# Coarser DMAs in a convolution kernel: stores and residual loads of three image pairs, and the last two pairs stored whole

## Chip, cores, metric

One core of one Trainium2 chip. The metric is device time in microseconds (us) of one execution. One run of the kernel before (211.6 us, slow) is left out by the comparison. A DMA is carried out by 16 DMA engines, here mostly in packets of 16 KB; it has landed when all 16 engines have sent their completion. Times inside an execution are counted from the start of the profiled span, which is 1.8 to 1.9 us shorter than the device time.

## The reference

A 3x3 convolution with padding 1 over 16 images of 64 channels and 64x64 pixels, plus a residual, all in float32.

```python
def reference(x, weight, residual):      # x (16,64,64,64), weight (64,64,3,3), residual (16,64,64,64)
    x_pad = np.pad(x, ((0, 0), (0, 0), (pad, pad), (pad, pad)), mode='constant')
    for b ...: for co ...: for ci ...: for kh ...: for kw ...:
        output[b, co] += weight[co, ci, kh, kw] * x_pad[b, ci, kh:kh+h, kw:kw+w]
    return (output + residual).astype(np.float32)
```

## The kernel before

Images go in pairs, 2 MB a pair, on 128 partitions. Three buffers (`xr`) take the loads of x. ScalarE casts every image in two halves into bfloat16 (`xp`, four buffers), TensorE convolves it into PSUM, and VectorE adds PSUM to the residual, which lies in one large tile (`ro`) for all eight pairs; the sum stays there and is stored from there. SyncE issues nearly all DMAs, in program order, on one queue.

```python
EARLY = (slice(0, 2), slice(2, 4), slice(4, 6), slice(6, 7))      # pairs stored while the work goes on
RES = (                                # pairs, columns, "issue behind the load of x pair ..."
    (slice(0, 1), WHOLE, None), (slice(1, 2), WHOLE, 1), (slice(2, 4), WHOLE, 3),
    (slice(4, 6), WHOLE, 5), (slice(6, 7), WHOLE, 7),
    (slice(7, 8), LEFT, 7), (slice(7, 8), RIGHT, 7),
)
# ... SyncE:
for p in range(NPAIR):
    if p >= NXR:                                        # NXR = 3 buffers
        nc.sync.wait_ge(s_half, 2 * (p - NXR) + 3)      # first cast of image 2*(p-3)+2 has ended
    load_x(p)                                           # (p == 0 goes to the front of the program)
    for i, (_, _, behind) in enumerate(RES):
        if behind == p:
            load_ro(i, nc.sync)
wait_ro(nc.sync, len(RES) - 2)                          # left half of residual pair 7 has landed
for pairs in EARLY:
    nc.sync.wait_ge(s_add, 2 * pairs.stop + 1)
    store(pairs).then_inc(s_out, 16)
# ... ScalarE, image n = 2p + im (cut):
i = nc.scalar.copy(out=t[64:128, 0:J, :], in_=x4[hp, :, 0, :])
i.then_inc(s_half, 1)
nc.scalar.copy(out=t[0:64, 1 : J + 1, :], in_=x4[hp, :, 1, :]).then_inc(s_pack, 1)
# ... at the very end, after all adds:
for cols in (LEFT, RIGHT):
    store(slice(NPAIR - 1, NPAIR), cols)
```

The load of x pair 7 (x7 below) reuses the buffer of pair 4, whose last reader is the second cast of image 9. But the counter `s_half` counts only first casts, so x7 waits for the first cast of image 10, which is the first image of pair 5. That cast can only run when x5 has landed.

Of the kernel before, what the change touches and what calls it, by code (L numbers as in the profile page):

```python
# [15 lines left out]
def kernel(  # L16
# [15 lines left out]
    NPAIR = B // 2  # L32
# [3 lines left out]
    NXR = 3  # L36
    NXP = 4
    NZERO = 4 + 2 * NXP
    EARLY = (slice(0, 2), slice(2, 4), slice(4, 6), slice(6, 7))
    WHOLE, LEFT, RIGHT = slice(0, NPIX), slice(0, NPIX // 2), slice(NPIX // 2, NPIX)  # L40
    RES = (
        (slice(0, 1), WHOLE, None),
        (slice(1, 2), WHOLE, 1),
        (slice(2, 4), WHOLE, 3),
        (slice(4, 6), WHOLE, 5),
        (slice(6, 7), WHOLE, 7),
        (slice(7, 8), LEFT, 7),
        (slice(7, 8), RIGHT, 7),
    )
# [40 lines left out]
    def wait_ro(e, i):  # L90
        e.wait_ge(s_r[i % NR], 16 * (i // NR + 1))

    def store(pairs, cols=slice(0, NPIX)):
        return nc.sync.dma_start(out=out_bc[:, pairs, cols], in_=ro[:, pairs, cols])
# [47 lines left out]
    with tc.tile_critical(no_gpsimd_drain=True):  # L142
# [14 lines left out]
        wait_ro(nc.sync, len(RES) - 2)  # L157
        for pairs in EARLY:
            nc.sync.wait_ge(s_add, 2 * pairs.stop + 1)
# [23 lines left out]
        for n in range(B):  # L183
            p, im = divmod(n, 2)
# [25 lines left out]
        for n in range(B):  # L210
            p, im = divmod(n, 2)
# [43 lines left out]
                m.then_inc(s_conv, 1)  # L255


    for cols in (LEFT, RIGHT):
        store(slice(NPAIR - 1, NPAIR), cols)
    with tc.tile_critical(sync_engine=mybir.EngineType.Pool, no_gpsimd_drain=True):  # L260
        nc.gpsimd.wait_ge(s_out, 16 * len(EARLY))
        tc.free_semaphores([s_w, *s_x, *s_r, s_out, s_id, s_half, s_pack, s_bank, s_conv, s_add])
# [30 lines left out]
```

## Time and profile before

| | |
|---|---|
| time | 122.21 us, median of 3 (122.2 to 122.54) |
| span of the profiled execution | 120.6 us |
| bytes | 33.70 MB read, 16.78 MB written, 22 DMAs |
| busy | PE 87.7 us, VectorE 76.0 us, ScalarE 63.1 us |

### The profile page before, as it was taken

The page shows a single profiled execution, that of the slowest core. Times are in us where ns is not written, and L with a number is a line of the kernel's source. Part 1 is how long each engine was busy: PE and PEld are TensorE (multiplying, and loading weights), DVE is VectorE, ACT ScalarE, POOL GpSimd, SP SyncE. Part 2 cuts the span into 40 slices and gives each one's busy share as a digit, 9 for nine tenths or more (in the row PEclk, how much of TensorE's full clock was granted, in tenths as well). Part 3 has the DMA queues.
Part 4 walks back from the last instruction along what each step waited for, and adds up shares of the span by engine and source line. Part 5 has one row for each costly group of instructions (what it writes and reads, how often), then busy time and mean ns, then how long its engine had stood idle before and what let it go on. Part 6 is the DMA issues. An engine that isn't in the chain of part 4 may idle for free.

```text
span 120.6 us, 734 instructions
## 1 busy us (share of the span) xinstructions
PE 87.7 (73%) x389; PEld 10.7 (9%) x105; DVE 76.0 (63%) x40; ACT 63.1 (52%) x37; POOL 2.4 (2%) x16
## 2 busy tenths in 40 slices
PE   0000609999999999999999999999999999400000
PEld 0000300111101110101010101010101010000000
DVE  0000080039898898988989898898988989890000
ACT  4001999999988595875959578595800000000000
POOL 5200000000000000000000000000000000000000
PEclk9999999999999999999999999999999999995555
DMA  7999999999999999999999999999999999999994
GB/s 239 429 424 429 430 429 429 429 435 435 435 429 429 424 429 424 429 435 424 435 429 435 435 435 418 421 459 435 429 429 429 429 429 435 435 435 429 399 427 168
DMA packets 3808, 50.48 MB, mean 419 GB/s; under 512 B 352, under 2 KB 480, under 8 KB 480
## 3 DMA queue, kind: packets, MB, share of 16 engines
q1 hardware_dynamic: 3664, 48.38, 94.2%
q10 hardware_dynamic: 144, 2.10, 4.1%
HBM read 33.70 MB, written 16.78 MB: 419 GB/s over the span
## 4 chain that ended last, share of the span: by engine, by line
PE 71%; DVEq 2%; DVE 2%; issue 0%
PE ps L101 54%; PE ps L100 17%; DVEq L142 2%; DVE ro L220 2%
## 5 line engine op out<-in xcount | busy, mean ns | idle before, releaser
L220 DVE TENSOR_TENSOR ro<-ps,ro 64x2048 f32<-64x2048 f32 x32 | 73.2, 2288 | 17.7 <-PE ps L101 17.2
L101 PE MATMUL ps<-xp,wl 128*128 128x504 bf16 (+1 forms) x288 | 80.0, 388 | 0.2
L190 ACT CAST xp<-xr 64x2048 bf16<-64x2048 f32 x16 | 30.3, 1896 | 22.5 <-PE ps L101 13.1
L100 PE MATMUL ps<-xp,wl 128*128 128x504 bf16 (+1 forms) x92 | 35.9, 390 | 3.4 <-PEq L241 3.4
L194 ACT CAST xp<-xr 64x2048 bf16<-64x2048 f32 x16 | 30.4, 1898 | 0.4
L100 PEld LDWEIGHTS ps<-xp,wl 128*128 128x128 bf16 x96 | 9.5, 99 | 79.1 <-issue 79.1
L206 DVE CAST wl<-ps 32x192 bf16<-32x192 f32 x8 | 2.8, 348 | 14.9 <-PE ps L233 14.8
L233 PE MATMUL ps<-ident,wraw 128*32 128x128 f32 x9 | 2.1, 412 | 12.6 <-DMA wraw<-in_weight_dram 12.6
L233 PEld LDWEIGHTS ps<-ident,wraw 128*32 128x32 f32 x9 | 1.2, 137 | 13.0 <-issue 12.6
L190 ACT ACT_TABLE_LOAD x1 | 1.3, 1283 | 1.1 <-SPq L142 1.1
L199 ACT CAST wl<-ps 32x192 bf16<-32x192 f32 x4 | 1.2, 306 | 0.0
L177 POOL MEMSET xp<- 64x64 bf16 x4 | 0.6, 146 | 0.2
L176 POOL MEMSET xp<- 64x64 bf16 x4 | 0.6, 144 | 0.2
L165 POOL TENSOR_SCALAR_AFFINE_SELECT ident<-ident 128x128 f32<-128x128 f32 x1 | 0.3, 292 | 0.2 <-POOL ident L163 0.2
L179 POOL MEMSET wl<- 64x192 bf16 x1 | 0.3, 253 | 0.1
L178 POOL MEMSET wl<- 64x192 bf16 x1 | 0.3, 251 | 0.1
L163 POOL MEMSET ident<- 128x128 f32 x1 | 0.2, 204 | 0.7 <-SPq L142 0.7
L277 POOL MEMSET const-bfloat16-1.0<- 128x1 bf16 x1 | 0.1, 111 | 0.0
L277 POOL MEMSET const-uint8-127<- 128x1 uint8 x1 | 0.1, 111 | 0.0
L277 POOL MEMSET const-float32-1.0<- 128x1 f32 x1 | 0.1, 108 | 0.0
L277 POOL MEMSET const-float32-0.0<- 128x1 f32 x1 | 0.1, 103 | 0.2 <-issue 0.2
## 6 DMA issues: line engine op xcount, KB each, us to landing
xr<-in_x_dram SPq DMA_DIRECT2D x8, 2048.0 KB, 14.4
out_dram<-ro SPq DMA_DIRECT2D x3, 4096.0 KB, 19.2
ro<-in_residual_dram SPq DMA_DIRECT2D x2, 4096.0 KB, 20.7
ro<-in_residual_dram SPq DMA_DIRECT2D x2, 2048.0 KB, 18.1
ro<-in_residual_dram ACTq DMA_DIRECT2D x1, 2048.0 KB, 12.0
ro<-in_residual_dram SPq DMA_DIRECT2D x2, 1024.0 KB, 18.8
out_dram<-ro SPq DMA_DIRECT2D x1, 2048.0 KB, 13.7
out_dram<-ro SPq DMA_DIRECT2D x2, 1024.0 KB, 9.4
```

The costliest lines, as they stand in the source:

```text
L100: return e.matmul(out=out_, lhsT=lhsT, rhs=rhs, start=start, stop=stop, skip_group_check=True)
L101: return e.add_instruction(mybir.InstMatmult(name=nc.get_next_instruction_name(), engine=PE, ins=[e.lower_ap(rhs), e.lower_ap(lhsT)], outs ...
L142: with tc.tile_critical(no_gpsimd_drain=True):
L176: nc.gpsimd.memset(t[0:64, 0, :], 0.0).then_inc(s_id, 1)
L177: nc.gpsimd.memset(t[64:128, J, :], 0.0).then_inc(s_id, 1)
L190: i = nc.scalar.copy(out=t[64:128, 0:J, :], in_=x4[hp, :, 0, :])
L194: nc.scalar.copy(out=t[0:64, 1 : J + 1, :], in_=x4[hp, :, 1, :]).then_inc(s_pack, 1)
L199: i = nc.scalar.copy(**weight_block(h, *b))
L206: i = nc.vector.tensor_copy(**weight_block(h, *b))
L220: i = nc.vector.tensor_tensor(out=o4[hp, :, par, :], in0=psj[64 * par : 64 * par + 64, :, :], in1=o4[hp, :, par, :], op=ADD)
L233: i = nc.tensor.transpose(out=tp[0:32, t // 3, 128 * (t % 3) : 128 * (t % 3) + 128], in_=wraw3[:, :, t], identity=ident[:, :])
L277: nc = _bacc.Bacc("TRN2", target_bir_lowering=False, num_devices=1)
```

## The change

The intent is fewer, larger DMAs on a kernel bound by transfers: 19 instead of 22.

```diff
-    EARLY = (slice(0, 2), slice(2, 4), slice(4, 6), slice(6, 7))
+    EARLY = (slice(0, 3), slice(3, 6))
@@ RES
         (slice(2, 4), WHOLE, 3),
-        (slice(4, 6), WHOLE, 5),
-        (slice(6, 7), WHOLE, 7),
+        (slice(4, 7), WHOLE, 4),
         (slice(7, 8), LEFT, 7),
         (slice(7, 8), RIGHT, 7),
@@ the end
-    for cols in (LEFT, RIGHT):
-        store(slice(NPAIR - 1, NPAIR), cols)
+    for p in range(NPAIR - 2, NPAIR):
+        store(slice(p, p + 1))
```

## The prediction

> **What bounds the kernel now.** I read the page first: busy shares, slices, DMA queues, the chain, then the groups. After that I read the SyncE queue's waits, the order of its issues, and stretches of the span with the DMA share.
>
> Page of the kernel before, slices and queue parts:
>
> ```profile
> span 120.6 us, 734 instructions
> ...
> PE   0000609999999999999999999999999999400000
> ...
> DMA  7999999999999999999999999999999999999994
> ...
> DMA packets 3808, 50.48 MB, mean 419 GB/s; under 512 B 352, under 2 KB 480, under 8 KB 480
> ```
>
> The reader is to see that the DMA row is full from the first slice to the last, while PE starts in slice 5 and ends in slice 35. Every one of the 50.48 MB is needed (33.70 MB read, 16.78 MB written), and at about 430 GB/s they take 117.4 us of the 120.6. PE's 87.7 us and VectorE's 76.0 us fit inside that. The page's chain names matmuls (71%), but it stops at 108.6 us, when the last add ends, and the span goes on for 12 us of pure stores. So I take the transfers as the bound, not the chain. The 352 packets under 512 B are the completion increments, 16 for each of 22 DMAs.
>
> Stretches of the span; columns are the stretch, its length, five engines' busy time, granted clock, DMA share and GB/s:
>
> ```profile
> 0.00:1.00 1.00, 0.00 (x0) 0.00 (x0) 0.00 (x0) 0.00 (x0) 0.21 (x4) 1.00 0.00 0
> 1.00:1.60 0.60, 0.00 (x0) 0.00 (x0) 0.00 (x0) 0.53 (x1) 0.26 (x2) 1.00 1.80 437
> 1.60:2.00 0.40, 0.00 (x0) 0.00 (x0) 0.00 (x0) 0.40 (x1) 0.34 (x2) 1.00 0.00 0
> 2.00:3.00 1.00, 0.00 (x0) 0.00 (x0) 0.00 (x0) 0.35 (x1) 0.73 (x6) 1.00 1.11 459
> ```
> ```profile
> 90.00:109.40 19.40, 13.90 (x64) 1.46 (x15) 16.73 (x8) 0.00 (x0) 0.00 (x0) 0.99 1.01 431
> 109.40:119.20 9.80, 0.00 (x0) 0.00 (x0) 0.00 (x0) 0.00 (x0) 0.00 (x0) 0.50 0.95 405
> 119.20:120.60 1.40, 0.00 (x0) 0.00 (x0) 0.00 (x0) 0.00 (x0) 0.00 (x0) 0.50 0.00 0
> ```
>
> A packet counts in the stretch in which it starts. The first load is issued at 0.00; its first packets start from about 1.0 to 1.6 us (the packet records say 1.03 on the first DMA engine and 1.56 on the last), and no second packet starts before 2.0. This is the only place in the trace where a transfer meets an empty queue. At the end packets stop at 119.2 and the last landing is 119.7.
>
> SyncE queue, two issues and the waits:
>
> ```profile
> 101.11 9.41 SPq L94 DMA_DIRECT2D out_dram<-ro  x3
> ```
> ```profile
> 108.88 1.65 SPq L94 DMA_DIRECT2D out_dram<-ro  x2
> ```
> ```profile
> SPq L82 <- ACT xp L190: 53.8, 5, 19.3
> SPq L94 <- DVE ro L220: 21.6, 2, 11.6
> SPq L94 <- DMA ro<-in_residual_dram: 16.6, 1, 16.6
> ```
>
> Pair 6 is stored at 101.11 and the two halves of pair 7 from 108.88, right after the last add (103.99 + 4.61 = 108.60 us in the timeline). SyncE waits often, but the DMA share shows that the queue held work through all these waits.
>
> **What the Trainium skill says.** (1) "DMA: Bandwidth & Descriptors", Specifications, puts the fabric ceiling of the 16 engines at 435 GB/s; the trace agrees, with 429 to 435 in most slices. (2) The same page, "Rules for kernel authors", asks for 128 partitions and at least 1 MiB per DMA. Every bulk DMA here has that already (1,024 KB is the smallest; the weights' 144 KB is the exception), so coalescing further has nothing left to win by this rule. (3) The same page, "Latency and other measured facts", gives about 600 ns to the first byte of such a DMA. The trace shows 1.0 to 1.6 us from issue to first packet at the cold start; I use the measured figure for the centre and the page's for the lower edge.
>
> **The change part by part.** No instruction of PE, VectorE, ScalarE or GpSimd changes; the ordering view shows only SyncE's list differing (apart from line numbers).
>
> *Fewer DMAs.* Three fewer completions. In the packet records a completion packet takes 9 ns, and a 16 KB packet 607 ns from start to start on one engine; the next data packet starts 6 ns after the completion. Three of them: about 0.02 us. Two 8 KB packets take 2 x 306 = 612 ns where one of 16 KB takes 607; a half pair is 8 such packets per engine, so storing pair 7 whole saves 8 x 5 = 0.04 us. Sum of the saving: 0.06 us. SyncE's issues cost 0.33 to 0.56 us each but lie beside transfers.
>
> *The residual load.* In the queue, x4 (issued 29.99) is now followed by residual pairs 4 to 6 (6 MB) and only then x5 (issued 38.48). Before, x4 was followed by x5. One pair (2 MB) takes 8 x 607 ns = 4.86 us on every engine. x4 lands at 29.99 + 16.6 = 46.6, as before. The 6 MB land at 46.6 + 14.6 = 61.2 (before, pairs 4 and 5 landed at 38.86 + 22.3 = 61.2 too), so the add of pair 4 at 67.68 has them. x5 lands at 66.0 instead of 38.48 + 13.0 = 51.5. ScalarE wanted it at 57.31, so its cast waits until 66.0 and ends the first image of pair 5 at 69.8. TensorE wants that image (number 10) at 26.19 + 9 x 5.19 = 72.9. Slack 3.1 us: a new ScalarE wait of 8.7 us, nothing on TensorE. Then x6 lands at 70.8; image 12's cast follows image 11's at 73.7, needed by 83.2. x7 may be issued when the first half of pair 5 is cast, at 66.0 + 1.9 = 67.9 (before: 59.23). Its first packets start at 68.9 to 69.5. x6's packets run until about 0.5 us before its landing, 70.4. So the queue keeps work with some 0.9 us to spare, x7 lands at 75.7 and the left residual half of pair 7, on which the stores wait, at 78.1, as before.
>
> *The early stores.* Pairs 0 to 2 go out at 78.2, with 1 MB of residual (2.4 us) still queued. Pairs 3 to 5 wait for the first add of image 12, exactly as pairs 4 and 5 did, so go out at 90.74. By then 12.5 us of the 2.4 + 14.6 us are done: 4.5 us of backlog, no gap. All six pairs have left the queue when they did before.
>
> *The last stores.* Here is the loss. The two last pairs are 16 packets of 607 ns per engine, 9.71 us. Counted back from 119.2, the queue has drained the first six pairs at 109.4 on its last engine (108.95 on its first, in the packet records). Before, pair 6 had been waiting in the queue since 101.11. Now pair 6 is issued with pair 7 after the last add, at 108.88. With 1.03 to 1.56 us to the first packet it starts at 109.9 to 110.4 where the engines are empty at 108.95 to 109.4: a hole of 1.0 us on every engine. At the cold start the first packet also held its engine for some 1.05 us instead of 0.61, a further 0.45; a store reading on-chip memory into a warm queue may be spared that, so I count half, 0.2. Sum: 1.0 + 0.2 - 0.06 = +1.15 us, all on the path that sets the end. 122.21 + 1.15 = 123.35 us.
>
> **The rivals.** *Fewer, larger DMAs help as intended.* For it: 22 become 19, two issues fewer among early stores. Against it: rates at 429 to 435 GB/s across the DMA boundaries, so there is no boundary cost to recover; it would make 122.1. *The issue is in time.* If the first packet follows within 0.6 us (the skill's figure), the hole is 0.6 or less and no slow first packet: about 122.6 to 122.8. *ScalarE starves TensorE.* If x5 came over 3.1 us later than I count, each further microsecond would delay the last add and, now that 4 MB wait for it, the end; even 2 us of it would give 125.4. Against it: x5's place in a full queue is fixed by bytes, and the full queue moves at one rate. *The queue runs dry before x7*, because its issue depends on the cast of x5: slack 0.9 us; a miss of 1 us would give 124.3 in all. *The queue refuses depth.* At 38.5 us some 11.5 MB are queued, more than before (about 9.5 MB); a blocked issue would still be behind a full queue, so costs nothing.
>
> **How the range follows.** No hole at all gives 122.15, the skill's latency 122.6, my count 123.35, a full slow first packet 123.6, and a hole at x7 besides 124.3. The runs before spread by 0.3. Range 122.4 to 124.2. Over 2% slower means above 124.65, which needs one of the two starvation rivals: 5%. Over 2% faster is below 119.8, hardly above the 117.4 us that the bytes need plus the start and the end: 1%.
>
> **What would show it.** Right: the DMA share dips below 1 near 109 to 110.5 us only, and last packets start near 120.3; SyncE's first late store is still issued at about 108.9; ScalarE shows a wait of 8 to 9 us on x5 from its load; TensorE's matmuls keep their 5.19 us step and the last add still ends near 108.6; SyncE's wait for the left residual half still ends near 78.2. Wrong: a zero in the DMA row near 69 us (x7 late), a TensorE wait near 73 us (x5 late), or no dip at 109 us (the issue was in time, or the earlier stores ran late). What would break the prediction is a later last add, or a warm issue much quicker or slower than the cold one.

## More of the kernel before

The page's row of transfer rates, for the kernel before, has 40 slices of 3 us each:

```profile
GB/s 239 429 424 429 430 429 429 429 435 435 435 429 429 424 429 424 429 435 424 435 429 435 435 435 418 421 459 435 429 429 429 429 429 435 435 435 429 399 427 168
```

From the second slice to the last but one it stays at 399 to 459 GB/s, mostly 424 to 435: the 16 DMA engines never stop. The DMA share of the prediction's fences says the same of the engines' time; this row says it of bytes.

## The result, and the profile after

The changed kernel takes 123.86 us (median of 6, 123.33 to 124.2), the kernel before in the same rounds 122.39 us. The ratio is 1.0119, 95% interval 1.0095 to 1.0144. (Ratios here are the mean time of one kernel's fast runs over that of the other's of the same rounds, so not quite the ratio of the medians quoted.) That is 1.46 us more, beside 1.15 forecast: less than 2%, but clear of the noise. The time lies inside the predicted range. The place of the loss does not.

The page of the changed kernel:

```profile
span 122.0 us, 731 instructions
...
DMA  7999999999999999999999999999999999999992
GB/s 231 424 430 424 430 430 430 430 430 430 430 430 430 430 430 430 430 430 440 430 435 430 430 365 395 422 408 430 430 430 430 430 430 430 430 430 430 435 430 107
DMA packets 3632, 50.48 MB, mean 414 GB/s; under 512 B 304, under 2 KB 432, under 8 KB 432
```

The 304 small packets are 16 completions for each of 19 DMAs, as intended. The DMA row shows no dip at all. The row of rates does: 365, 395, 422 and 408 GB/s from 70 to 82 us, and nothing near 109 us, where the prediction had put the hole. Stretches of both kernels narrow it down (columns as in the prediction: stretch, length, five engines' busy time, granted clock, DMA share, GB/s). First before, then after:

```profile
70.00:74.00 4.00, 3.95 (x20) 0.39 (x4) 3.42 (x2) 2.63 (x2) 0.00 (x0) 1.00 1.04 446
109.20:110.40 1.20, 0.00 (x0) 0.00 (x0) 0.00 (x0) 0.00 (x0) 0.00 (x0) 0.50 1.02 437
```
```profile
66.00:70.00 4.00, 4.00 (x21) 0.43 (x5) 3.39 (x3) 3.83 (x3) 0.00 (x0) 1.00 0.99 426
70.00:74.00 4.00, 3.95 (x19) 0.45 (x5) 3.42 (x2) 3.95 (x3) 0.00 (x0) 1.00 0.99 365
74.00:78.00 4.00, 4.00 (x21) 0.49 (x5) 3.39 (x3) 3.95 (x3) 0.00 (x0) 1.00 0.98 410
...
109.20:110.40 1.20, 0.00 (x0) 0.00 (x0) 0.00 (x0) 0.00 (x0) 0.00 (x0) 0.50 1.02 437
```

From 70 to 74 us the engines are "busy" 0.99 of the time and yet move 365 GB/s instead of 446. Their packets have become longer, up to 1.73 us instead of 0.61 (below), and a packet counts as busy for its whole length. PE's busy time in the stretch is the same 3.95 us, so TensorE did not starve. At 109.2 us both kernels move 437 GB/s: no hole.

What is transferred from 70 us is x7. The SyncE queue's issue of x7 and its time to landing (min, median and max of the one DMA), before and then after:

```profile
59.23 0.33 SPq L82 DMA_DIRECT2D xr<-in_x_dram  x1
...
DMA to landing us min/median/max: 11.7/11.7/11.7
```
```profile
68.04 0.33 SPq L81 DMA_DIRECT2D xr<-in_x_dram  x1
...
DMA to landing us min/median/max: 9.3/9.3/9.3
```

Before, x7 landed at 59.23 + 11.7 = 70.9 us; after, at 68.04 + 9.3 = 77.3 us. In the new order it should have landed one pair (4.86 us) after x6, which landed at 70.9 us, so at 75.8. It came 1.5 us late. All that follows is shifted: the left half of residual pair 7 landed at 79.8 us instead of 78.2, and the last store at 121.1 instead of 119.7.

The reason for the issue at 68.04 us is in ScalarE's timeline of the changed kernel: the cast of image 10 waited 10.94 us for x5, and ended at 66.12 + 1.90 = 68.02 us.

```profile
66.12 1.90 ACT L189 CAST xp<-xr 64x2048 bf16<-64x2048 f32 x1 [10.94 <-DMA xr<-in_x_dram]
```

In the packet records (one row per packet, with its start and length) the last packets of x6 end at 70.1 to 70.5 us on the 16 engines. So x7 was issued 2.1 to 2.5 us before the queue would run out. Ten engines took its first packet at once at the usual 611 ns. The other six took 0.86 to 1.73 us over their first or second packet, two of them after 0.3 and 0.8 us of idleness. At 72.6 to 73.8 us the ten had a slow packet too, their fifth, of 0.86 to 1.06 us. I call the time from an issue to the end of what stands before it in the queue its **lead**.

### The profile page after: what moved, and what is told of

It reads as the page before. It is cut to its first block, busy times and chain, and to the rows that moved or that the text cites. A ratio compares the mean times of both kernels' runs of the same rounds, so it can differ in the third digit from the quotient of the medians.

```text
span 122.0 us, 731 instructions
## 1 busy us (share of the span) xinstructions
PE 86.9 (71%) x389; PEld 10.7 (9%) x105; DVE 76.0 (62%) x40; ACT 63.1 (52%) x37; POOL 2.4 (2%) x16
## 4 chain that ended last, share of the span: by engine, by line
PE 70%; DVEq 2%; DVE 2%; issue 0%
PE ps L100 53%; PE ps L99 17%; DVEq L141 2%; DVE ro L219 2%
```

## The experiments

Two theories stood at the start. **T**: x7 is issued with too little lead, and its packets come late. **L**: the loss is the hole before the last stores, as the prediction had it. T carried a doubt: whether it is the lead, or something else about that stretch, the order, or what is issued beside it. "Before" was 122.37 to 122.47 us in all rounds.

### The two halves of the change alone

`e1_res_only` is the kernel before with the new `RES` only; `e2_store_only` is the changed kernel with the old `RES`.

```diff
# e1_res_only, against before            # e2_store_only, against before
-        (slice(4, 6), WHOLE, 5),        -    EARLY = (0:2, 2:4, 4:6, 6:7)
-        (slice(6, 7), WHOLE, 7),        +    EARLY = (0:3, 3:6)
+        (slice(4, 7), WHOLE, 4),        and pairs 6 and 7 stored whole at the end
```

> The kernel before with the residual loads of the change only (one load of three pairs behind x4); the stores stay those of before, with pair 6 queued early and pair 7 in halves. Theory T (the load of x7 is issued only 2.1 us before the queue runs out, because it waits for a cast of x5, and several DMA engines get its packets late): the whole loss is here, ratio 1.010 to 1.013, x7 lands near 77.3 us instead of 75.7 and the DMA row dips near 70 to 74 us. Theory L (the last stores are issued too late, the prediction's hole): ratio 1.000, 0.0 to 0.1 us below before, no dip anywhere.

> The changed kernel with the residual loads of before, so only the stores are changed. Theory T: no dip at 70 to 74 us; the queue then drains the first six pairs near 109.0 to 109.4 us, and the issue of pair 6 at 108.1 to 108.9 decides whether a hole opens that the loss at x7 had hidden in the changed kernel: 0.2 to 1.0 us, ratio 1.002 to 1.008. Theory L with the prediction's size: a hole of 1.0 to 1.2 us near 109 to 110.5 us, ratio 1.008 to 1.010.

Measured: e1 124.18 us, ratio 1.0146 (1.0131 to 1.0161); e2 122.63 us, ratio 1.0022 (1.0007 to 1.0036). Stretches of e1, then of e2:

```profile
70.00:74.00 4.00, 3.95 (x19) 0.49 (x5) 3.39 (x3) 3.95 (x3) 0.00 (x0) 1.00 0.95 320
```
```profile
70.00:74.00 4.00, 3.95 (x20) 0.43 (x5) 3.42 (x2) 2.63 (x2) 0.00 (x0) 1.00 1.04 446
...
109.20:109.50 0.30, 0.00 (x0) 0.00 (x0) 0.00 (x0) 0.00 (x0) 0.00 (x0) 0.50 0.01 0
109.50:110.40 0.90, 0.00 (x0) 0.00 (x0) 0.00 (x0) 0.00 (x0) 0.00 (x0) 0.50 1.37 583
```

The residual load alone makes the whole loss, and a little more (1.8 us; x7 landed at 77.7 us there, and its slowest packets took 2.2 to 2.3 us). L falls as the cause in the changed kernel. In e2, however, the predicted hole is there: no data packet starts from 109.2 to 109.5 us. Pair 6 was issued at 108.66 us, its first packets start at 109.50 to 109.66, 0.84 to 1.0 us later, and they take their usual 0.61 us, with no slow first packet. The engines that finished last were idle for 0.12 to 0.28 us only, and the last landing came 0.13 us later than before. In the changed kernel, x7's loss had moved the end of the first six pairs to 109.9 to 111.1 us, behind the issue at 108.12, so that this hole was covered. The two losses do not add: 1.8 and 0.26 us alone, 1.46 together.

### More lead for x7

`e3_x7_free` lets x7 go by the buffer's true last reader: the second cast of image 9 also raises `s_half`, and a copy of 64 elements onto itself takes over raising `s_pack`. `e4_halves_first` leaves the issue where it is and puts the two residual halves ahead of x7.

```diff
# e3_x7_free, against the changed kernel
-            nc.scalar.copy(out=t[0:64, 1 : J + 1, :], in_=x4[hp, :, 1, :]).then_inc(s_pack, 1)
+            i = nc.scalar.copy(out=t[0:64, 1 : J + 1, :], in_=x4[hp, :, 1, :])
+            if n == 9:
+                i.then_inc(s_half, 1)
+                i = nc.scalar.copy(out=t[0:64, J, :], in_=t[0:64, J, :])
+                i._wait_ge(s_half, 11)
+            i.then_inc(s_pack, 1)
# e4_halves_first, against the changed kernel
-        (slice(7, 8), LEFT, 7), (slice(7, 8), RIGHT, 7),
+        (slice(7, 8), LEFT, 6), (slice(7, 8), RIGHT, 6),
```

(A first form of e3 that raised two semaphores by one instruction did not compile.)

> The changed kernel, with x7 released by the second cast of image 9 (near 56 us, the last reader of its buffer) instead of the first cast of image 10 (near 68 us); ScalarE gets one extra copy of 64 elements for it. Theory T: x7 has 14 us of lead, no dip at 70 to 74 us, x7 lands near 75.8, and the time is that of e2_store_only within 0.1 us. If the slow packets near 70 to 74 us come from something else in that stretch (the order of the loads, the adds, the memory): they stay, ratio 1.010 to 1.013.

> The changed kernel, with the two residual halves of pair 7 issued ahead of x7 instead of behind it. x7 is still issued near 68 us, but 2 MB (4.9 us) more stand before it, so its lead is 7 us instead of 2.1. Theory T: no dip at 70 to 74 us, all loads have landed near 80.6, time that of e3_x7_free within 0.1 us. If the late issue as such costs (and not the short lead), the loss of 1.4 us stays, ratio 1.010 to 1.013.

Measured: e3 122.48 us, ratio 1.0016 (0.9999 to 1.0033); e4 122.87 us, ratio 1.0048 (1.0035 to 1.0061). Stretches of e3, then of e4:

```profile
70.00:74.00 4.00, 3.95 (x19) 0.39 (x4) 3.42 (x2) 3.95 (x3) 0.00 (x0) 1.00 1.06 455
```
```profile
70.00:74.00 4.00, 3.95 (x19) 0.39 (x4) 3.42 (x2) 3.95 (x3) 0.00 (x0) 1.00 0.99 418
77.00:80.00 3.00, 3.00 (x16) 0.29 (x3) 2.42 (x2) 2.95 (x3) 0.00 (x0) 1.00 1.01 371
```

In e3 x7 runs in the same stretch, in the same order, beside the same casts as in the changed kernel, only issued at 54.94 us, and its packets are all 611 ns. So neither the order nor what runs beside x7 is enough for the loss; what is left is the time of issue, of x7 and of the two residual halves that follow it. e3 keeps the late stores of the change, yet shows no hole before them: pair 6 was issued at 107.85 us, 1.1 to 1.5 us before the queue would run out, and its packets follow without a gap at 0.61 us. (Its time is 0.15 us under that of e2, where 0.1 was expected.) e4 missed its expectation: x7 begins well with 7 us of lead, and then has slow packets at the end, from 78 us. That is a second effect, followed below.

### How much lead

Three kernels hold x7 of e3 back by an additional wait on a constant: the first add of image 7, the fifth weight group of image 8, and the first add of image 8.

```diff
                 nc.sync.wait_ge(s_half, 2 * (p - NXR) + 3)
+                if p == NPAIR - 1:
+                    nc.sync.wait_ge(s_add, 8)     # e5_lead5;  e8_lead0: (s_add, 9);  e10_lead3: (s_mid, 3)
```

> As e3_x7_free, but x7 is held back until the first add of image 7 (near 64.8 us), so its lead over the end of x6 (70.1 to 70.5 us) is 5.3 us; the two residual halves follow it at once, as in the changed kernel. Theory T (a load needs some lead, more than the 2.1 us of the changed kernel): if 5 us are enough, no slow packets of x7 and the time of e3_x7_free within 0.2 us (122.5); if they are not, a part of the 1.4 us stays (122.8 to 123.8). Theory U (whatever is issued near 65 to 69 us is slow, whatever its lead): 123.5 or more.

> As e5_lead5, but x7 is released by the fifth of the six weight groups of image 8 (near 66.6 us), a lead of 3.4 to 3.8 us between the 5.8 us that cost nothing and the 2.1 to 2.5 us that cost 1.5 us. In the changed kernel the slow engines reached full pace 3.2 to 4.1 us after the issue. Theory T with that figure: a loss of 0 to 0.7 us, 122.4 to 123.1, with few or no slow first packets of x7. If the loss hardly depends on the lead up to some threshold (0.3 us of lead cost 1.6, 2.3 us cost 1.5): 1.2 to 1.6 us, 123.6 to 124.0.

> As e5_lead5, but x7 is held back until the first add of image 8 (near 70.0 us), which leaves a lead of 0.1 to 0.5 us. Theory T with the late packets of the changed kernel (3.2 to 4.1 us after the issue on the slow engines) whatever the queue does: loss of 3.0 to 3.7 us, 125.5 to 126.0. If an emptied queue takes up a load as at the cold start (first packets 1.03 to 1.56 us after the issue and 0.5 us longer than usual): loss of 1.2 to 2.0 us, 123.7 to 124.4, so hardly more than the changed kernel lost with 2.1 us of lead.

x6 landed at 70.8 to 70.95 us in all five, so the following differ in the issue of x7, and of the two residual halves, which follow it within 0.9 us in each. The lead runs from the issue to the end of x6's packets on the first and the last engine.

| kernel | x7 issued | lead, us | x7 landed | median time, us | ratio to before |
|---|---|---|---|---|---|
| e3_x7_free | 54.94 | 15 | 75.7 | 122.48 | 1.0016 (0.9999 to 1.0033) |
| e5_lead5 | 64.32 | 5.7 to 6.2 | 75.8 | 122.52 | 1.0006 (0.9991 to 1.0021) |
| e10_lead3 | 66.53 | 3.5 to 3.9 | 75.7 | 122.41 | 1.0004 (0.9988 to 1.0019) |
| changed kernel | 68.04 | 2.1 to 2.5 | 77.3 | 123.86 | 1.0119 (1.0095 to 1.0144) |
| e8_lead0 | 69.86 | 0.1 to 0.6 | 77.5 | 123.95 | 1.0122 (1.0095 to 1.0149) |

Stretches of e5, e10 and e8, in this order:

```profile
70.00:74.00 4.00, 3.95 (x19) 0.49 (x5) 3.42 (x2) 3.95 (x3) 0.00 (x0) 1.00 1.02 438
```
```profile
70.00:74.00 4.00, 3.95 (x19) 0.49 (x5) 3.42 (x2) 3.95 (x3) 0.00 (x0) 1.00 1.05 451
```
```profile
70.10:70.80 0.70, 0.70 (x5) 0.10 (x1) 0.70 (x1) 0.70 (x1) 0.00 (x0) 1.00 0.01 0
...
70.00:74.00 4.00, 3.95 (x20) 0.41 (x5) 3.42 (x2) 3.95 (x3) 0.00 (x0) 1.00 0.85 262
```

The lead is the cause, and the loss is not proportional to it. From 3.5 us up there is none. At 2.1 to 2.5 us it is as large as at 0.1 to 0.6, as far as the spread of these two kernels (0.9 us each) lets one see. In e8 the queue really empties (no data packet starts from 70.1 to 70.8 us); the first packets start 0.96 to 1.41 us after the issue and take up to 1.78 us. With 2.1 us of lead there is hardly any idle engine, and the same 1.5 us go into slow packets. The form of T that put 3.2 to 4.1 us after every issue (125.5 us for e8) is wrong: a load taken up by an emptied queue is quicker than that.

### The second effect: stores queued behind the last load

`e6_halves_first_free` is e4 with x7 issued early. `e9_stores_held` is e6 with the stores held back. `e7_x7_alone_late` is e6 with x7 issued late and nothing behind it.

```diff
# e9_stores_held, against e6                 # e7_x7_alone_late, against e6
         wait_ro(nc.sync, len(RES) - 2)      +  x7 waits: nc.sync.wait_ge(s_conv, 10)
+        nc.sync.wait_ge(s_half, 15)         +  first store waits: nc.sync.wait_ge(s_add, 11)
```

> e4_halves_first with x7 issued near 56 us as in e3_x7_free; the order in the queue is that of e4 (x6, the two halves, x7), and the stores go out at 73.2 us as in e4, 7 us ahead of their turn. e4 had slow packets at the end of x7, near 78 to 80 us, worth 0.3 to 0.5 us. If they came of x7's late issue (lead 7 us), they are gone here: 122.5. If they came of stores queued behind x7 or of x7 as the last load: they stay, 122.8 to 123.0.

> e6_halves_first_free, with the first store held back until the first cast of image 13 (near 79.5 us), so that nothing stands behind x7 in the queue while its packets run; x7 has long been queued. In e6 the last packets of x7 ran at half pace on all engines from 77.4 to 80.2 us, with three pairs of stores queued behind them since 73.3 us, and cost 0.6 us. If the queued stores cause that: x7 lands at 80.6, packets all near 611 ns, and the time is 122.4 to 122.7 (a store hole of 0 to 0.4 us included). If it is x7 as the last load or its place near 78 us: the slow packets stay, 122.9 to 123.4.

> As e6, but x7 is issued at 72.9 us (end of the convolution of image 9), 2.1 to 2.4 us ahead of its turn, and with nothing issued behind it: the stores wait for the first add of image 10 (80.4 us). Theory T: x7's packets are slow as in the changed kernel, landing 1.0 to 1.6 us later than without (81.5 to 82.1 instead of 80.5). Theory V (the two issues right behind x7 delay its packets, not its short lead): x7 lands at 80.5 to 80.8. In either case a hole follows before the stores, unless x7 ends later than their first packet, near 81.3 us; so total 123.6 to 124.3 for T, 123.2 to 123.6 for V.

Measured: e6 122.98 us, ratio 1.0049 (1.0034 to 1.0063); e9 122.85 us, ratio 1.0044 (1.0029 to 1.0059); e7 123.52 us, ratio 1.0072 (1.0040 to 1.0103), with a wide spread, 122.69 to 123.93. The time of e9 lies between its two expected ranges, and that of e7 in the range of the theory against T. So what follows rests on the packets of one profiled execution of each, the slowest of four for e6 and e7 and the fastest for e9. Stretches of e6, then of e9:

```profile
77.00:80.00 3.00, 3.00 (x16) 0.29 (x3) 2.85 (x2) 2.95 (x3) 0.00 (x0) 1.00 0.96 300
```
```profile
77.00:80.00 3.00, 3.00 (x15) 0.39 (x4) 2.52 (x2) 2.95 (x3) 0.00 (x0) 1.00 0.89 382
80.00:80.40 0.40, 0.40 (x4) 0.00 (x0) 0.40 (x1) 0.40 (x1) 0.00 (x0) 1.00 0.10 41
```

In e6 x7 has 20 us of lead and still slow packets from 77.4 to 80.2 us, of up to 1.3 us on all engines; it landed at 81.5 us. Three pairs of stores had stood behind it since 73.3 us. In e9 they came at 79.47 us, every packet of x7 took 611 ns, and it landed at 80.5. (Its 382 GB/s is the queue running out: a packet counts where it starts, and none of x7 starts after 79.56 us.) e4, with the stores behind x7 too, shows the slow packets in its fastest execution and landed x7 at 81.1. So the 0.6 to 1 us comes with the stores waiting behind the last load; why, no run here shows. In e9 the packets of x7 end from 79.7 to 80.2 us and the store's begin at 80.4 to 80.55, 0.9 to 1.1 us after the issue, so that e9 pays part of the gain back as a hole, and its total hardly moves. (In the kernel before and in e3, the stores are issued at 78.1 to 78.2 us, 1.6 to 2 us before the packets of the last load half end, and neither the hole nor the slow packets are seen.)

e7 puts x7 at a lead of about 2 us without any issue behind it before 80.66 us. It landed at 81.4 us, 0.9 us later than in e9, with slow packets (0.74 to 1.45 us) on ten engines before 77.5 us. From 72 to 77 us e7, then e9:

```profile
72.00:77.00 5.00, 4.95 (x23) 0.48 (x5) 4.39 (x3) 4.95 (x3) 0.00 (x0) 1.00 1.02 408
```
```profile
72.00:77.00 5.00, 4.95 (x24) 0.53 (x6) 4.58 (x2) 4.95 (x3) 0.00 (x0) 1.00 1.03 436
```

So the short lead costs without the two issues that follow x7 in the changed kernel; whether these add the rest of the 1.5 us there is open. Its store, issued at 80.66 us, shows its first packets at 81.59 to 81.73, 0.93 to 1.07 us later, again of normal length. They start 1.2 us later than in e9, and the last landing comes 1.2 us later too (121.2 against 120.0 us). So e7's time is set by its late store and says nothing for or against T; only the landing of x7 does, which was expected at 81.5 to 82.1 us for T and at 80.5 to 80.8 against it.

### Both holes closed, and a third term

`e11_both` is e3 with pair 6 stored early by itself again. `e12_both_halves` is e11 with pair 7 stored in two halves, as before.

```diff
# e11_both, against e3                                   # e12_both_halves, against e11
-    EARLY = (slice(0, 3), slice(3, 6))                  -    for p in range(NPAIR - 1, NPAIR):
+    EARLY = (slice(0, 3), slice(3, 6), slice(6, 7))     -        store(slice(p, p + 1))
-    for p in range(NPAIR - 2, NPAIR):                   +    for cols in (LEFT, RIGHT):
+    for p in range(NPAIR - 1, NPAIR):                   +        store(slice(NPAIR - 1, NPAIR), cols)
```

> The changed kernel with both of its holes closed: x7 released early as in e3_x7_free, and pair 6 stored by itself ahead of the end as in the kernel before; pair 7 stays whole, so 20 DMAs. If the two causes are all there is: before's time within 0.1 us, ratio 0.999 to 1.001, the two DMAs fewer being worth nothing (0.05 us by the packet records).

> e11_both with pair 7 stored in two halves again, as in the kernel before (21 DMAs). In e11 the last packets landed at 119.48 us, 0.2 us ahead of before, but the span ended 1.52 us after that landing instead of 0.91 (120.6 less 119.70), because GpSimd's clean-up of the semaphores waits for the first of the last stores, and there was only one: in before it ran beside the right half. If that is the cause: the end is again 0.9 us after the last landing, and the time is 122.2 to 122.5, ratio 0.998 to 1.001. If something else in e11 cost the 0.6 us (the early store of pair 6 beside the large ones): 122.9 stays.

Measured: e11 122.96 us, ratio 1.0045 (1.0032 to 1.0059), against the expectation; e12 122.42 us, ratio 0.9997 (0.9983 to 1.0011). SyncE queue's waits at the end, e11 and then e12:

```profile
SPq L292 <- POOLq L264: 12.1, 1, 12.1
```
```profile
SPq L292 <- DMA out_dram<-ro: 10.1, 2, 7.7
```

In e11 SyncE's last wait is ended by GpSimd, in e12 by the stores. GpSimd clears the semaphores at the end once the first of the last stores has landed. With two last stores that runs beside the second one (117.3 to 118.1 us in the kernel before). With a single one it comes after all data: e11's last landing is at 119.48 us, earlier than before's 119.70, but its span ends 1.6 us after the landing instead of 0.9. So the halves of pair 7 were worth some 0.6 us (0.54 between the medians), for a reason that has nothing to do with transfers. The change kept two last stores, so it didn't pay this.

e12, with 20 DMAs and the three-pair transfers of the change, is the kernel before in time. (The page counts 320 small packets in e12 and 304 in e11, 16 for each DMA, so 20 and 19 DMAs; the expectations, with 21 and 20, miscount by one.) No version beat it: with the holes closed, two DMAs fewer are worth nothing that these runs resolve.

## Why the prediction was right in its time and wrong in its mechanism

- **The bound**: right. Outside the lost stretch every slice but the first and the last moves 424 to 440 GB/s in the changed kernel (before: 399 to 459).
- **Fewer DMAs worth 0.06 us**: consistent with e12 (0.9997, within 0.0014 of nothing). Nothing finer is shown.
- **ScalarE waits for x5, TensorE doesn't**: right. x5 landed at 66.0 us as worked out, the wait grew to 10.94 us (8.7 forecast; the rest is mostly the 1.37 us that this cast had waited for TensorE before, and 0.76 us by which ScalarE ran ahead in this execution), PE's busy time from 70 to 74 us stayed 3.95 us, and the last add ended at 107.84 us (before 108.60).
- **"the queue keeps work with some 0.9 us to spare, x7 lands at 75.7"**: this step failed. The issue came at 68.04 us, as forecast (67.9), but I took the time to the first packet's start, 1.03 to 1.56 us from the cold start, as all that a load needs. Measured, 2.1 to 2.5 us of lead still cost 1.5 us and 3.5 us cost nothing. The rival "the queue runs dry before x7" had named the place and was dismissed on that number. I had even seen the cold start's slow first packets and charged them to the store, not to this load.
- **"a hole of 1.0 us on every engine" before the last stores, and 0.2 us of slow first packets**: mis-sized where it can be seen, in e2, and absent in the changed kernel. A store's first packets came 0.84 to 1.07 us after the issue and were never slow. The engines that finish last, which set the end, were idle for 0.12 to 0.28 us, and the total was 0.26 us instead of 1.2. When the last add ends matters too: over the 14 profiled executions the last stores were issued between 107.6 and 109.1 us without relation to the change.
- **The sum** came out near by luck: one loss was put in for another of like size. What told them apart was the list of signs: it asked for a dip at 109 to 110.5 us "only". The dip was at 70 to 74 us, and the wait for the left residual half ended at 79.8 us instead of near 78.2.
- **The sign "DMA share dips"** was the wrong instrument: the share stayed at 0.99 while bytes per second fell from 446 to 365 GB/s. The rate has to be read.

## What to carry to other kernels

In this stream, bound by transfers, 20 DMAs, all but the weights of 1 to 6 MB, took as long as 22; what mattered was that every issue came early enough. The one load that was tested by steps needed more lead (over 2.5 us, with 3.5 us enough) than a store (1.1 us was enough in e3). When loads are reordered, follow the chain of buffer releases to the next issues: a larger load put ahead of x5 delayed x5's cast, and through a counter that released the buffer later than its last reader, x7's issue by 9 us. Read the rate beside the busy share, and leave some small work, such as a last half store, for the end's housekeeping to hide behind.

## What the Trainium skill lacked or had wrong

- "DMA: Bandwidth & Descriptors", Latency and other measured facts, gives about 600 ns to the first byte of a DMA issued from SyncE. These runs show 0.84 to 1.07 us from issue to the start of a store's first packets in a drained queue (e2, e7, e9), and 0.96 to 1.56 us for loads (cold start, e8), whose first packets then take up to 1.78 us instead of 0.61.
- The same page's "Rules for kernel authors" says to issue a DMA early; it has no lead for an issue into a queue that is still working. Here 2.1 to 2.5 us cost 1.5 us, and 3.5 to 3.9 us nothing.
- "Perfetto Trace Analysis", DMA Engine Tracks, says that slices show actual busy time. That section does not add that slow packets fill this time without moving more: a share of 0.99 went with 365 GB/s in the changed kernel, where 1.04 went with 446 GB/s before. (Under "Identifying the Most-Contended Engine" the page itself calls the occupancy of the DMA engines misleading; these runs agree.)
- No page that I read has it that stores queued early behind the last load slow that load's last packets (e6 against e9: up to 1.3 us instead of 0.61, landing 1 us later, one profiled execution each). The mechanism is open.
- No page that I read has it that the semaphore clean-up at the end can hide behind the last of two stores (e11 against e12: 0.6 us).
